# Layer 1's first pass reads x a second time with columns on partitions; the norm's roots are spread by a matmul of ones with a diagonal

## The chip, the cores and the metric

One core of one Trainium2 chip runs the whole kernel. The time is device microseconds of one execution; lower is better. The engines are named as the profile names them: PE is TensorE's matmul stream, PEld its weight loads, DVE is VectorE, ACT is ScalarE, POOL is GpSimd, SP is SyncE, which issues the DMAs.

## What is computed

A trunk of two layers over 2048 positions of width 1024, all in float32. Only the start of layer 1 matters here:

```
h = rms_norm(x, a_norm_g)          # x * rsqrt(mean(x*x) + 1e-6) * g, per position
u, v, z = split(h @ w_in, 3)       # w_in is 1024 x 6144
```

After that come a gated mixing over chunks, an output projection, and a second layer with chunked attention. The change leaves all of that alone.

## The kernel before, in words

**Products.** A float32 product is written as three products of float32r halves: `mm3` (L110 to L114) multiplies high by high (L111), high by low (L112) and low by high (L113). `split` (L433) makes the halves: ACT casts the high half (L434), DVE subtracts it from the source to get the low half (L437). Each large product is a 2x2 block scheme with seven partial products, numbered `ph`, in the order `PH = (1, 2, 6, 5, 7, 4, 3)`.

**Steps.** Layer 1's input projection runs in steps `(n, ph, j)`: `n` is one of six column groups of `w_in`, `ph` a partial product, `j` one of eight pairs of row blocks (x has 16 blocks of 128 rows; block 2j is the upper one of pair j, block 2j+1 the lower). A step is one 128x512 product of 12 matmuls. In the first pass, `n == 0`, steps 0 to 15 (`ph` 1 and 2) do the product for `n` 0 and `n` 1 together, so 24 matmuls each; steps 16 to 55 do `ph` 6, 5, 7, 4, 3 with 12 each. `run_steps` (L659) walks the steps; at each step it runs the events of that step, then the products (`act`), then prepares the left operand of the step three later (`prep`, `LOOK = 3`), then the list `ts` (weight loads and weight sums). This order of the program gives priorities; the framework's scheduler sets the order on each engine from them, so an instruction can stand some places away from where the source has it. Every engine then works through its queue in order.

**Left operands of the first pass.** `block_norm` (L692) makes a normalised block of 128 rows in four parts: `load` (SP reads x, and once the gains `gab` copied to all partitions), `square` (ACT, L703, sum of squares by row), `power` (DVE adds epsilon, L709; POOL raises to -1/2, L710) and `scale` (DVE, L714, one instruction of 128x1024: row factor and gains). `block_a(j)` does it for block 2j into `ha`, `block_b(j)` for block 2j+1 into `hb`. `block_c` (L728) forms the sums of the scheme on POOL (L734 to L736); `prep0` forms one more (L753). Rows are on partitions, but a matmul needs columns of x on partitions, so `s_split` (L607) turns each half block with four TensorE transpositions into PSUM tile `t0` (L611), then splits that tile into a tile `S`. It also stores `S` to the scratch `hsd` in DRAM (L614), from which later phases reload it (L602). `s_split` is called for all seven `ph` and eight `j`: 56 times.

**What sets the order around it.** `norm_at` (L915) places the parts of a block at steps: `load` early, `square` and `power` at step s, `scale` at s+1. The first two blocks are done ahead of all (`first_two`); blocks `ha` 2 to 7 load at once, `hb` blocks follow every 7/4 steps. `block_c` comes 2 and `block_d` 4 steps after the square of `hb`. All DMAs go through SP's queue in order: x loads (L697), weights `rw` (L470), stores `hsd` (L614), stores `vd` of finished v (L638), reloads of `S` (L602). POOL also sums weight blocks for the scheme (`comb`, L445). Finished products leave PSUM by `evict` (L568): ACT copies for `ph` 1 (L574), DVE adds for the others (L570). 32 dummy matmuls (L879) run before the first product.

Of the kernel before, what the change touches and what calls it, by code (L numbers as in the profile page):

```python
# [9 lines left out]
F32 = mybir.dt.float32  # L10
F32R = mybir.dt.float32r
BF16 = mybir.dt.bfloat16
AF = mybir.ActivationFunctionType
# [4 lines left out]
P = 128  # L18
# [15 lines left out]
def trunk_kernel(  # L34
    ctx: ExitStack,
    tc: tile.TileContext,
    x: bass.AP,
    a_norm_g: bass.AP,
    w_a: bass.AP,
    ln_g: bass.AP,  # L40
# [343 lines left out]
    with ExitStack() as actx:  # L384
# [48 lines left out]
        def split(hi, lo, src, key=None):  # L433
            ins = nc.scalar.copy(hi, src)  # L434
            if key:
                in_order(key, ins)
            nc.vector.tensor_tensor(lo, src, hi.bitcast(F32), op=sub)  # L437
            return ins
# [167 lines left out]

        def s_split(ph, j, rows):  # L607

            pt = ptp[0].tile([P, 4, P], F32, tag="t0", name=f"t0_{ph}_{j}", bufs=4)
            for k in range(4):  # L610
                tpose(pt[:, k, :], rows[:, k * P : k * P + P], ident[:])  # L611
# [76 lines left out]
        gab = p0.tile([P, D], F32, name="gab")  # L688
        ha = {}
        h21 = {}  # L690

        def block_norm(blk, t):  # L692

            r = sm.tile([P, 1], F32, tag="rr", name=f"ra{blk}", bufs=4)

            def load():
                nc.sync.dma_start(t, x[blk * P : (blk + 1) * P, :])  # L697
                if blk == 0:
                    nc.sync.dma_start(gab[:], a_norm_g.partition_broadcast(P))

            def square():
                jk = ca.tile([P, D], BF16, tag="acc", name=f"jk{blk}", bufs=25)
                ins = nc.scalar.activation(  # L703
                    jk[:], t, AF.Square, scale=1.0 / 32, accum_out=r[:]
                )
                last["square"] = ins.ins.name

            def power():
                nc.vector.tensor_scalar(r[:], r[:], EPS, None, op0=add)  # L709
                ins = nc.gpsimd.tensor_tensor(r[:], r[:], mhalf[:], op=ALU.pow)  # L710
                last["power"] = ins.ins.name

            def scale():
                nc.vector.scalar_tensor_tensor(t, t, r[:], gab[:], op0=mul, op1=mul)  # L714

            return load, square, power, scale

        def block_a(j):
            h = ha[j] = p0.tile([P, D], F32, tag="ha", name=f"ha{j}", bufs=8)
            return block_norm(2 * j, h[:])  # L720

        hb = {}

        def block_b(j):
            h = hb[j] = p0.tile([P, D], F32, tag="hb", name=f"hb{j}", bufs=3)
# [12 lines left out]
        def block_d(j):  # L738
            s_split(5, j, hb.pop(j)[:, 0:512])
# [150 lines left out]
        def at(s, f_):  # L890
            events.setdefault(s, []).append(f_)
# [23 lines left out]
        def norm_at(load, s, block, j):  # L915
            todo = []

            def first():
                todo.extend(block(j))
                todo.pop(0)()  # L920

            ts.setdefault(load, []).append(first)
# [356 lines left out]
    with ExitStack() as bctx:  # L1279
# [716 lines left out]
```

## Time and profile before

| | us |
|---|---|
| median of 3 runs | 2656.24 |
| lowest and highest run | 2654.09, 2656.88 |
| span of the profiled execution, first to last instruction | 2652.0 |
| PE busy in it | 2608.0 |
| DVE, ACT, POOL busy | 1885.1, 1303.2, 897.2 |

The profile is one execution. It gives its span, not a device time of its own; the runs shown lie 2.1 to 4.9 us above that span. A busy time is the sum of the durations of an engine's instructions; matmuls overlap in their pipeline, so PE's real pace is read from the distance between the starts of two instructions in the timeline, not from a duration. In the timeline a row is: start, length, engine, line, operation, output and input, count; in brackets the idle time before it and what ended it.

### The profile page before, as it was taken

Reading aid. Unit: us, or ns where it says so; the run is one execution under the profiler, and the core shown is the slowest. Engines: PE = TensorE matmul, PEld = TensorE weight load, DVE = VectorE, ACT = ScalarE, POOL = GpSimd, SP = SyncE. Lnnn points to the kernel's source line nnn. Section 1 sums busy time; section 2 is a strip of 40 time slices with the busy share of each in tenths; the row PEclk is TensorE's granted clock in tenths of the full one; section 3 lists DMA queues with packets and bytes.
Section 4 is the critical chain, followed back from the end, with each engine's and each line's share of the span. In section 5 each row is a group of like instructions: output and inputs, shape, how many; then the busy total and the mean of one; then the engine's idle time right before and its main releaser. Section 6 shows DMA issues by size and latency. Waiting matters only on the chain. (4 is left out here: it accounts for less than half of the span.)

```text
span 2652.0 us, 37980 instructions
## 1 busy us (share of the span) xinstructions
PE 2608.0 (98%) x12960; PEld 2181.4 (82%) x12960; DVE 1885.1 (71%) x2944; ACT 1303.2 (49%) x2303; POOL 897.2 (34%) x874
## 2 busy tenths in 40 slices
PE   8999999999999999999989999999999999999997
PEld 7888888888888888888878878888888888888886
DVE  5655676865767667757767767777778777877677
ACT  5422243442533434343356456666666655666564
POOL 3611334142152322203234434344332232332245
PEclk9999999999999999999999999999999999999999
DMA  7898998989989869967776597778787666875667
GB/s 286 313 344 329 346 370 323 323 323 338 330 302 313 308 233 324 331 206 270 280 251 214 186 280 229 231 245 263 252 270 254 226 204 224 255 230 161 195 224 251
DMA packets 273856, 718.72 MB, mean 271 GB/s; under 512 B 28800, under 2 KB 68736, under 8 KB 273664
## 3 DMA queue, kind: packets, MB, share of 16 engines
q1 hardware_dynamic: 273664, 716.31, 78.4%
q8 instruction: 103, 1.69, 0.3%
q14 instruction: 89, 0.73, 0.1%
HBM read 531.12 MB, written 174.59 MB: 266 GB/s over the span
## 5 line engine op out<-in xcount | busy, mean ns | idle before, releaser
L111 PE MATMUL P<-T,S 128*128 128x512 f32 x1248 | 496.2, 398 | 2.1 <-ACT S L434 2.1
L112 PE MATMUL P<-T,S 128*128 128x512 f32 x1248 | 488.2, 391 | 1.1 <-DVE T L437 1.1
L113 PE MATMUL P<-T,S 128*128 128x512 f32 x1248 | 488.6, 391 | 0.0
L1417 POOL TENSOR_SCALAR pr<-pr,sl 128x640 f32<-128x640 f32 (+4 forms) x256 | 209.7, 819 | 530.4 <-DVE sl L1416 445.2
L111 PE MATMUL pj<-hh_b,wh_b 128*128 128x512 f32 x768 | 320.4, 417 | 0.0
L113 PE MATMUL pj<-hh_b,wl_b 128*128 128x512 f32 x768 | 305.0, 397 | 1.2 <-DVE wl_b L229 1.1
L112 PE MATMUL pj<-hl_b,wh_b 128*128 128x512 f32 x768 | 303.4, 395 | 0.1
L1413 ACT ACTIVATE pr<-pr,nm 128x640 f32<-128x640 f32 (+4 forms) x256 | 195.5, 764 | 188.1 <-DVE nm L1406 186.6
L113 PEld LDWEIGHTS P<-T,S 128*128 128x128 f32 x1248 | 234.9, 188 | 50.5
L111 PEld LDWEIGHTS P<-T,S 128*128 128x128 f32 x1248 | 235.5, 189 | 46.9 <-ACT S L434 2.3
L112 PEld LDWEIGHTS P<-T,S 128*128 128x128 f32 x1248 | 235.6, 189 | 46.1 <-DVE T L437 1.3
L1438 DVE TENSOR_TENSOR pt<-tp,pt 128x640 fp32r<-128x640 f32 (+4 forms) x256 | 188.4, 736 | 43.7 <-ACT pt L1437 41.1
L1406 DVE CUSTOM_DVE_ANT_0 pr<-s,bias 128x640 f32<-128x640 f32 (+4 forms) x256 | 187.9, 734 | 35.7 <-PE s L1398 29.8
L1437 ACT CAST pt<-tp 128x640 fp32r<-128x640 f32 (+4 forms) x256 | 159.0, 621 | 54.0 <-PE tp L1433 49.8
L1433 PE MATMUL tp<-ident,pr 128*128 128x128 f32 x1120 | 166.7, 275 | 8.6 <-DVE pt L1438 7.3
L113 PEld LDWEIGHTS pj<-hh_b,wl_b 128*128 128x128 f32 x768 | 144.7, 188 | 36.4 <-DVE wl_b L229 3.8
L1433 PEld LDWEIGHTS tp<-ident,pr 128*128 128x128 f32 x1120 | 130.7, 140 | 43.3 <-issue 13.7
L111 PEld LDWEIGHTS pj<-hh_b,wh_b 128*128 128x128 f32 x768 | 145.8, 190 | 18.1 <-ACT wh_b L228 1.6
L1458 PEld LDWEIGHTS pv<-pt,V 128*128 128x128 f32 x896 | 143.3, 189 | 20.8 <-DVE pt L1438 3.9
L112 PEld LDWEIGHTS pj<-hl_b,wh_b 128*128 128x128 f32 x768 | 145.8, 190 | 17.1 <-DVE hl_b L186 0.6
L1458 PE MATMUL pv<-pt,V 128*128 128x256 f32 (+3 forms) x896 | 154.5, 320 | 2.2 <-ACT pt L1437 1.1
L229 DVE TENSOR_TENSOR wl_b<-raw_b,wh_b 128x1024 fp32r<-128x1024 f32 x96 | 120.4, 1255 | 28.5 <-ACT wh_b L228 27.8
(294 smaller groups left out, 5725.9 us busy)
## 6 DMA issues: line engine op xcount, KB each, us to landing
S<-hsd SPq DMA_DIRECT2D x288, 512.0 KB, 5.3
rw<-in_w_a SPq DMA_DIRECT2D x108, 512.0 KB, 6.3
A<-ytd SPq DMA_DIRECT2D x72, 512.0 KB, 5.7
raw_b<-wk SPq DMA_DIRECT2D x72, 512.0 KB, 4.3
hsd<-S SPq DMA_DIRECT2D x56, 512.0 KB, 4.9
V<-vhd SPq DMA_DIRECT2D x56, 512.0 KB, 5.4
bias<-reld SPq DMA_DIRECT2D x64, 320.0 KB, 4.2
va<-vd SPq DMA_DIRECT2D x32, 512.0 KB, 5.5
```

The costliest lines, as they stand in the source:

```text
L111: first = mm(ps, lh, rh, start=first, stop=False)
L112: mm(ps, lh, rl, start=False, stop=False)
L113: mm(ps, ll, rh, start=False, stop=last)
L229: tv(wl[:], raw[:], wh[:].bitcast(F32), op=sub)
L1406: nc.vector.tensor_tensor_reduce(out=pr[:, c0:].rearrange("p (a b) -> p a b", a=nseg), in0=ps[:, :nseg, :w], in1=bias[:, c0:].rearrange("p ...
L1413: nc.scalar.activation(pr[:, c0:], pr[:, c0:], AF.Exp, scale=-1.0, bias=nm[:], accum_out=sl[:])
L1417: nc.gpsimd.tensor_scalar(pr[:, c0:], pr[:, c0:], sl[:], 1.0, op0=ALU.mult, op1=ALU.mult)
L1433: ins = tpose(tp[:, b, :], pr[:, b * P : (b + 1) * P], ident[:])
L1437: nc.scalar.copy(oh, tp[:, b0:5, :].rearrange("p a b -> p (a b)"))
L1438: nc.vector.tensor_tensor(pt[:, 2560 + o + b0 * P : 2560 + o + 640], tp[:, b0:5, :].rearrange("p a b -> p (a b)"), oh.bitcast(F32), op=ALU ...
L1458: mm(po[:, q0 * P : q1 * P], vtl[t, p][:, i, hs], rhs, start=(i == blocks[0] and j == 0), stop=(i == 7 and j == 1),)
```

## The change

The host hands over a second copy of x, `xt`, in which each block of 128 rows is stored with columns on partitions: partition p holds, for k = 0 to 7, column 128k + p of the block's 128 rows. The gains come as 128 x 8, column on partition.

- `s_split` no longer transposes: it splits the half block straight from SBUF. The tile `t0` and the 56 x 4 transpositions are gone.
- `square` still works on x with rows on partitions, since it sums along a row. For `ha` blocks 0 to 3 that copy of x goes to a tile of its own (`xn`, of the tag of `hb`, now 4 buffers for 3) and SP loads `xt` beside it. For the other 12 blocks x is loaded into the block's tile, squared, and then ACT issues a DMA that overwrites the tile with `xt`.
- The row factors must now lie along the free axis. After the -1/2 power, POOL scales the identity by them (`dg`, a 128x128 diagonal); `spread`, new, is one float32 matmul of a tile of ones with `dg`, which leaves in PSUM tile `rb` the 128 factors on every partition.
- `scale` is eight DVE instructions of 128x128 for one of 128x1024: block column k of the tile times its gain times `rb`.
- `norm_at` gets a place for `spread`, and `scale` comes one step later for blocks not made ahead; `block_c` and `block_d` move one step later with it.

```diff
         def s_split(ph, j, rows):
-            pt = ptp[0].tile([P, 4, P], F32, tag="t0", name=f"t0_{ph}_{j}", bufs=4)
-            for k in range(4):
-                tpose(pt[:, k, :], rows[:, k * P : k * P + P], ident[:])
             t = s_tile(f"S0_{ph}_{j}")
-            split(t[:, 0], t[:, 1], pt[:], "S")
+            split(t[:, 0], t[:, 1], rows.rearrange("p (k c) -> p k c", k=4), "S")
...
-        def block_norm(blk, t):
+        def block_norm(blk, t, xr=None):
             r = sm.tile([P, 1], F32, tag="rr", name=f"ra{blk}", bufs=4)
+            apart = xr is not None
+            xr = t if xr is None else xr
+            dg, rb = [], []
             def load():
-                nc.sync.dma_start(t, x[blk * P : (blk + 1) * P, :])
                 if blk == 0:
-                    nc.sync.dma_start(gab[:], a_norm_g.partition_broadcast(P))
+                    nc.sync.dma_start(ga[:], a_norm_g)
+                nc.sync.dma_start(xr, x[blk * P : (blk + 1) * P, :])
+                if apart:
+                    nc.sync.dma_start(t, xt[blk])
             def square():
...
+                if not apart:
+                    nc.scalar.dma_start(t, xt[blk])
             def power():
...
+                dg.append(p0.tile([P, P], F32, tag="dg", name=f"dg{blk}", bufs=2))
+                nc.gpsimd.tensor_scalar(dg[0][:], ident[:], r[:], 1.0, op0=mul, op1=mul)
+            def spread():
+                rb.append(ptp[0].tile([P, P], F32, tag="rb", name=f"rb{blk}", bufs=2))
+                mm(rb[0][:], ones[:], dg[0][:], start=True, stop=True)
             def scale():
-                nc.vector.scalar_tensor_tensor(t, t, r[:], gab[:], op0=mul, op1=mul)
+                for k in range(KD):
+                    c = slice(k * P, k * P + P)
+                    nc.vector.scalar_tensor_tensor(
+                        t[:, c], t[:, c], ga[:, k : k + 1], rb[0][:], op0=mul, op1=mul
+                    )
...
             ts.setdefault(load, []).append(first)
-            at(s, lambda: todo.pop(0)())
-            ts.setdefault(s, []).append(lambda: todo.pop(0)())
-            at(s + 1, lambda: todo.pop(0)())
+            at(s, one)
+            ts.setdefault(s, []).append(one)
+            if s < -1:
+                at(s + 1, one)
+                at(s + 1, one)
+            else:
+                ts.setdefault(s + 1, []).append(one)
+                at(s + 2, one)
...
-            at(e + 2, lambda j=j: block_c(j))
-            at(e + 4, lambda j=j: block_d(j))
+            at(e + 3, lambda j=j: block_c(j))
+            at(e + 5, lambda j=j: block_d(j))
```

More of the change, by code (lines that the diff above doesn't have):

```diff
@@ L687, in trunk_kernel @@
         ptp = [ptx.enter_context(tc.tile_pool(name="pt0", bufs=1, space=PSUM))]
-        gab = p0.tile([P, D], F32, name="gab")
+        ga = p0.tile([P, KD], F32, name="ga")
+        ones = p0.tile([P, P], F32, name="ones")
+        nc.gpsimd.memset(ones[:], 1.0)
         ha = {}
         h21 = {}
-        def block_norm(blk, t):
+        def block_norm(blk, t, xr=None):
             r = sm.tile([P, 1], F32, tag="rr", name=f"ra{blk}", bufs=4)
+            apart = xr is not None
+            xr = t if xr is None else xr
+            dg, rb = [], []
             def load():
-                nc.sync.dma_start(t, x[blk * P : (blk + 1) * P, :])
                 if blk == 0:
-                    nc.sync.dma_start(gab[:], a_norm_g.partition_broadcast(P))
+                    nc.sync.dma_start(ga[:], a_norm_g)
+                nc.sync.dma_start(xr, x[blk * P : (blk + 1) * P, :])
+                if apart:
+                    nc.sync.dma_start(t, xt[blk])
             def square():
@@ L711, in power, with hb_tile @@
                 last["power"] = ins.ins.name
-            def scale():
-                nc.vector.scalar_tensor_tensor(t, t, r[:], gab[:], op0=mul, op1=mul)
-            return load, square, power, scale
+                dg.append(p0.tile([P, P], F32, tag="dg", name=f"dg{blk}", bufs=2))
[3 more added lines that the diff above has]
+                mm(rb[0][:], ones[:], dg[0][:], start=True, stop=True)
+            def scale():
+                for k in range(KD):
[3 more added lines that the diff above has]
+                    )
+            return load, square, power, spread, scale
+        def hb_tile(name):
+            return p0.tile([P, D], F32, tag="hb", name=name, bufs=4)
         def block_a(j):
             h = ha[j] = p0.tile([P, D], F32, tag="ha", name=f"ha{j}", bufs=8)
-            return block_norm(2 * j, h[:])
+            return block_norm(2 * j, h[:], hb_tile(f"xn{j}")[:] if j < 4 else None)
         hb = {}
         def block_b(j):
-            h = hb[j] = p0.tile([P, D], F32, tag="hb", name=f"hb{j}", bufs=3)
+            h = hb[j] = hb_tile(f"hb{j}")
             return block_norm(2 * j + 1, h[:])
@@ L1967 @@
         "x": c(a["x"][0]),
-        "a_norm_g": c(a["a_norm_g"][0]),
+        "xt": c(a["x"][0].reshape(S // P, P, KD, P).transpose(0, 3, 2, 1).reshape(S // P, P, D)),
+        "a_norm_g": c(a["a_norm_g"][0].reshape(KD, P).T),
         "w_a": c(np.stack([quarters(m) for m in w_a])),
```

5 lines of the change are left out of this document (4 added, 1 removed).

## Prediction

> **What bounds the kernel now.** I read the page first, then the table of engines by stretches of time around the change, then the line of the transpositions with its timeline, and last the waits of the engines that feed TensorE there.
>
> ```profile
> span 2652.0 us, 37980 instructions
> PE 2608.0 (98%) x12960; PEld 2181.4 (82%) x12960; DVE 1885.1 (71%) x2944; ACT 1303.2 (49%) x2303; POOL 897.2 (34%) x874
> ```
>
> ```profile
> 0.00:10.00 10.00, 7.10 (x36) 6.66 (x36) 1.64 (x4) 4.34 (x6) 2.09 (x10) 1.00 0.77 281
> 10.00:28.00 18.00, 16.11 (x69) 12.63 (x69) 14.56 (x19) 14.54 (x27) 2.75 (x5) 0.91 1.01 398
> 28.00:40.00 12.00, 11.65 (x59) 9.66 (x59) 8.14 (x10) 4.55 (x9) 9.67 (x8) 1.00 0.12 46
> 40.00:56.00 16.00, 11.96 (x56) 9.95 (x55) 8.65 (x11) 8.46 (x14) 5.74 (x6) 0.89 0.98 357
> 56.00:72.00 16.00, 16.00 (x82) 13.38 (x81) 7.93 (x11) 8.38 (x15) 7.49 (x7) 1.00 0.77 292
> 72.00:88.00 16.00, 16.00 (x82) 13.41 (x81) 9.46 (x14) 8.95 (x16) 15.06 (x12) 1.00 0.85 305
> 88.00:104.00 16.00, 16.00 (x85) 13.49 (x83) 11.62 (x18) 4.85 (x9) 12.23 (x11) 1.00 0.73 241
> 104.00:122.00 18.00, 18.00 (x90) 15.00 (x89) 13.35 (x20) 9.76 (x16) 10.18 (x7) 1.00 0.95 359
> 170.00:236.00 66.00, 66.00 (x309) 54.56 (x308) 47.00 (x67) 24.05 (x36) 10.11 (x8) 1.00 0.93 323
> ```
>
> After the stretch come PE, PEld, DVE, ACT and POOL busy, then the clock, the DMA share and GB/s. TensorE is the bound: from 56 us on it is never idle, while DVE has a third of its time free. Only before 56 us does it wait. So an instruction taken out of TensorE's queue behind 56 us is time won, as long as nothing else becomes late. Two things are near their end: POOL in 72 to 88 (15.06 of 16) and the DMAs, whose highest rate here is 398 GB/s.
>
> **Removed: 224 transpositions.**
>
> ```profile
> L611 PE MATMUL t<-ident,ha x128: 270/272/328, 8.1 to 233.8; 128*128 128x128 f32 x128
> L611 PE MATMUL t<-ident,hb x64: 272/273/447, 28.5 to 123.0; 128*128 128x128 f32 x64
> L611 PE MATMUL t<-ident,h x32: 270/272/273, 147.3 to 170.1; 128*128 128x128 f32 x32
> ```
>
> ```profile
> 55.88 0.40 PE L111 MATMUL P<-T_hh,S 128*128 128x512 f32 x1
> ...
> 58.39 0.39 PE L113 MATMUL P<-T_hh,S 128*128 128x512 f32 x1
> 58.62 0.60 PE L611 MATMUL t<-ident,ha 128*128 128x128 f32 x4
> 58.97 0.48 PE L111 MATMUL P<-T,S 128*128 128x512 f32 x1
> 59.29 0.40 PE L112 MATMUL P<-T,S 128*128 128x512 f32 x1
> ```
>
> The durations (0.27) overlap, so I take starts. From 55.88 to 58.39 lie 11 steps of one matmul: 0.228 each. From 58.39 to 59.29 lie 0.90, in which two such steps (0.456) are matmuls; the other **0.444** is the group of four transpositions. 128 + 64 + 32 are 224, that is 56 groups: 56 x 0.444 = **24.9 us** of TensorE.
>
> **Added on TensorE: 16 matmuls of ones with a diagonal.** No float32 matmul that isn't a transposition or a float32r half stands in this trace. From below, it costs as much as one transposition of the same 128 columns, 0.444 / 4 = 0.111. From above, 0.74, what the slow group of four below takes from its start to the next. I take 0.4: the kernel itself needs three products of halves for one float32 product, and four transpositions (0.444) are the nearest row to three passes with their weight loads. 16 x 0.4 = **6.4 us** (1.8 to 11.8). The Trainium skill, "TensorE: Matmul & The Clock Gate", section "Terms", says the transpose mode is four times faster for FP32 than a matmul. By it each would cost 0.444, an estimate, and the sum below would be 0.7 us later; no row here shows it.
>
> **Added beside TensorE.**
>
> ```profile
> L714 DVE SCALAR_TENSOR_TENSOR ha<-ha,ra,gab x8: 1276/1285/2303, 6.8 to 36.6; 128x1024 f32<-128x1024 f32 x8
> L807 DVE SCALAR_TENSOR_TENSOR va<-va,lmv,lg x64: 732/745/1855, 348.0 to 933.4; 128x512 f32<-128x512 f32 x64
> L1438 DVE TENSOR_TENSOR pt<-tp,pt 128x128 fp32r<-128x128 f32 x16 | 4.6, 285 | 0.3
> L1417 POOL TENSOR_SCALAR pr<-pr,sl 128x128 f32<-128x128 f32 x16 | 6.8, 426 | 8.0 <-DVE sl L1416 7.3
> L437 DVE TENSOR_TENSOR S<-t,S 128x512 fp32r<-128x512 f32 x56 | 37.1, 685 | 13.0 <-ACT S L434 13.0
> ```
>
> DVE: eight operations of 128x128 with one operand in PSUM, like L1438, 0.285 each, so 2.3 for 1.285 (between 1.6 at 0.2 and 2.9 at 0.36, which L714 and L807 give when their line is drawn on to 128 columns). That is 1.0 more per block, 16 us in all, nearly all between 10 and 122 us, where the quoted stretches leave DVE 38 us free: nothing, except in 10 to 28 (14.56 of 18), which I count below. The low halves of `S` (0.685) read two SBUF tiles instead of PSUM and SBUF. L714, which did so before, stretches from 1.285 to 2.303 at worst; such stretching leaves the scale and comes to the 56 splits. I set it at nothing: DVE has the room. POOL: 16 diagonals at 0.426 are 6.8 us; hidden on average, not in 72 to 88.
>
> ```profile
> hb<-in_x SPq DMA_DIRECT2D x8, 512.0 KB, 6.6
> ```
>
> ACT: 12 DMA issues, each behind the square whose tile it overwrites. The square is the instruction ahead on the same engine, so the casts and copies behind wait little, and ACT is half idle from 56 us on. But each of these transfers starts only then, and DVE's first scale waits for it; behind that scale stand the adds that empty PSUM, and behind those TensorE. An x block took 6.6 us to land; square and scale are two steps apart, 24 matmuls or 5.5 us each. So 11 us cover 6.6, and this costs nothing while transfers stay under that. `block_c` and `block_d` come a step later, and with them their `hsd` stores in SP's queue; their tiles are first used in step 24 (`ph` 5), so nothing waits.
>
> **Start.** Before the first product SP loaded x, gains, x; now it loads x, xt, x, xt, so the weights come one 512 KB load later: 0.524 MB at 398 GB/s, 1.3 us. The chain of the first block loses a group of transpositions (0.44) and the wait for `gab` below, and gains the diagonal (0.43), the matmul (0.4) and 1.0 of scale.
>
> ```profile
> 6.76 1.28 DVE L714 SCALAR_TENSOR_TENSOR ha<-ha,ra,gab 128x1024 f32<-128x1024 f32 x1 [1.09 <-DMA gab<-in_a_norm_g]
> 10.82 0.50 PE L111 MATMUL P<-T,S 128*128 128x512 f32 x1 [2.07 <-ACT S L434]
> ```
>
> That is +0.3 for the chain beside +1.3 for the loads, and DVE now has two longer scales ahead of the first low halves. I take **+2 us** (-1, if the 1.09 is all that counts, to +5, if the two further xt loads of this stage, 2.6, push as well).
>
> **The DMAs.** Sixteen xt blocks less the `gab` copy are 15 x 0.524 = 7.9 MB, at 398 GB/s 19.8 us of transfers, before 122 us. The quoted DMA shares leave 24.5 us free there (10.6 of them in 28 to 40, at share 0.12). But 32 groups lie in that part, so it gets 32 x 0.444 - 6.4 = 7.8 us shorter: 16.7 us are left for 19.8. I count the missing **3 us** as waits of TensorE (0 to 13.6, below).
>
> **The stall that is there.**
>
> ```profile
> 51.10 1.09 PE L611 MATMUL t<-ident,hb 128*128 128x128 f32 x4 [4.04 <-DVE hb L714]
> 51.84 0.78 PE L111 MATMUL P<-T,S 128*128 128x512 f32 x1
> 52.41 0.63 PE L112 MATMUL P<-T,S 128*128 128x512 f32 x1
> ...
> 54.50 0.40 PE L111 MATMUL P<-T,S 128*128 128x512 f32 x1
> ```
>
> ```profile
> 45.43 1.05 ACT L434 CAST T<-rw 128x1024 fp32r<-128x1024 f32 x1 [10.35 <-DMA rw<-in_w_a]
> ```
>
> TensorE waited 4.04 for a normalised `hb`, then ran slowly: 51.10 to 52.41 is 1.31 where 58.62 to 59.29 is 0.67, and the five steps to 54.50 take 2.09 for 1.14, so 1.6 more. The block was late since its square stood on ACT behind a cast that waited 10.35 for weights. The transposition that waited goes, but the new matmul of the same block stands behind the same square. I leave this stall as it is (0 to -5.6).
>
> **Sum.** -24.9 + 6.4 + 2 + 3 = **-13.5 us**. The profiled span of 2652.0 becomes 2638.5; the median lies 4.2 above that span, and with that kept the forecast is **2642.7 us**.
>
> **Rivals.**
>
> ```profile
> POOL ra L710: 17.2, 14
> 36.59 2.30 DVE L714 SCALAR_TENSOR_TENSOR ha<-ha,ra,gab 128x1024 f32<-128x1024 f32 x1 [2.40 <-POOL ra L710]
> 91.36 1.28 DVE L714 SCALAR_TENSOR_TENSOR hb<-hb,ra,gab 128x1024 f32<-128x1024 f32 x1 [6.34 <-POOL ra L710]
> 106.00 1.06 ACT L703 ACTIVATE jk<-hb 128x1024 bf16<-128x1024 f32 x1 [4.54 <-DMA hb<-in_x]
> ```
>
> *Slower: TensorE waits for the roots.* Before, DVE's scale waited for the root, 17.2 us in 14 waits, up to 6.34 where POOL was full, and TensorE went on with other products. Now the matmul that spreads the roots stands in TensorE's own queue; behind it stand products that need nothing of it. If those 17.2 us and the 4.54 for `hb` become TensorE's, with three slow restarts at 1.6, that is 26.5 us: -13.5 + 26.5 gives **2669 us**. It decides from 18.8 us of such waits on. Against it: the matmul comes a step, some 5.5 us, behind the root in the program, more than all waits but one.
>
> *No difference: the DMAs have no room.* The free 10.6 us of 28 to 40 were free because SP's queue stood still; if it does so again and only ACT's few loads use them, 13.6 us are missing instead of 3: -24.9 + 6.4 + 2 + 13.6 = -2.9, **2653 us**. For it: 398 and 357 GB/s on both sides of the gap. Against it: ACT's DMAs do not stand in SP's queue. The Trainium skill, "DMA: Bandwidth & Descriptors", section "Issuing engines are not separate DMA queues", states that a second issuing engine saves only issue time, since all share the same 16 engines; that speaks for this rival, and this trace, with one hardware queue, cannot show it.
>
> *More gain.* The matmul costs as little as a transposition (1.8 for 16), the stall with its slow restart goes (5.6), no DMA is late: -24.9 + 1.8 + 2 - 5.6 = -26.7, **2629.5 us**.
>
> **How the numbers follow.** Forecast 0.50, slower 0.20, no difference 0.13, more gain 0.17. A measurement of this kernel tells some 0.2% from no change, 5.3 us. The forecast with its own bounds (2634 to 2652) gives nearly all to faster, 0.03 to no difference: faster 0.64, same 0.16, slower 0.20. The range runs from 2627, which takes in the larger gain and its lower bounds, to 2667, where the rival on the other side has most of its price; some 0.18 is left out.
>
> **What would show it.** Right: no L611; in steps without waits one product of 12 matmuls follows the other with no gap of 0.44; the ones matmul at 0.4 from start to start; TensorE still full from about 60 us. Wrong: idle time of PE in front of the spread matmul with POOL's `dg` as releaser (first rival); casts or scales that wait for `xt` or `rw` with DMA share near 1 (second); a first product later than 13 us. The size fails if the ones matmul costs much over 0.74, or if DVE's eight operations take over 2.9 and the low halves come late.

## The result and the profile after

| | us |
|---|---|
| changed kernel, median of 6 runs | 2670.16 (2662.77 to 2677.24) |
| kernel before, median of 6 runs beside them | 2656.56 (2654.09 to 2660.67) |
| ratio, with its 95% interval | 1.0051 [1.0038, 1.0065] |
| span of the profiled execution, changed and before | 2665.9 and 2652.0 |

The change makes the kernel 0.5% slower, 13.6 us. The forecast was 2642.7. The rival "Slower: TensorE waits for the roots" had named 2669; how much of that agreement is luck is said further down.

The page of the changed kernel, its head:

```profile
span 2665.9 us, 37763 instructions
PE 2596.3 (97%) x12768; PEld 2167.2 (81%) x12768; DVE 1912.5 (72%) x3056; ACT 1304.8 (49%) x2303; POOL 908.7 (34%) x891
```

TensorE has 192 instructions less (224 transpositions gone, 32 new: each matmul of ones is two) and 11.7 us less busy time, but the span is 13.9 longer. So it idles more. Its stretches of time, with columns as before:

```profile
10.00:28.00 18.00, 11.50 (x43) 8.59 (x44) 13.90 (x39) 10.78 (x16) 2.48 (x6) 0.81 1.00 391
28.00:40.00 12.00, 11.50 (x55) 9.22 (x54) 9.75 (x39) 9.20 (x19) 4.96 (x10) 1.00 0.99 356
...
56.00:72.00 16.00, 11.83 (x43) 9.32 (x43) 13.64 (x24) 7.49 (x13) 11.22 (x8) 0.79 0.77 281
72.00:88.00 16.00, 16.00 (x74) 13.23 (x73) 6.94 (x17) 8.98 (x15) 11.34 (x11) 1.00 0.77 290
88.00:104.00 16.00, 12.05 (x50) 9.57 (x50) 16.00 (x27) 5.82 (x11) 9.42 (x9) 0.93 0.87 311
104.00:122.00 18.00, 12.91 (x51) 10.36 (x50) 12.84 (x23) 7.92 (x13) 17.92 (x14) 0.88 0.84 306
...
170.00:236.00 66.00, 57.86 (x245) 46.54 (x244) 45.99 (x62) 22.90 (x34) 17.41 (x13) 0.97 0.91 330
```

Where TensorE had been full from 56 us on, it now has holes: 11.83 of 16, 12.05 of 16, 12.91 of 18, 57.86 of 66. In the second of these stretches DVE is busy all the time, in the third POOL nearly so (17.92 of 18). The clock falls below 1 in the same stretches. The idle DMA time of 28 to 40 us (share 0.12 before) is used: 0.99. What TensorE waited for in the first 330 us:

```profile
PE rb L724 <- POOL dg L720: 18.0, 7, 5.1
PE P L112 <- DMA S<-hsd: 8.4, 5, 3.4
PE P L112 <- ACT S L435: 5.3, 2, 5.1
```

Total, number of waits, longest. Before, no `S` reloaded from `hsd` was late and there were no diagonals. The third row is the start: 5.06 of it stands in front of the first product. Of the 18.0 for the diagonals, 2.8 lie there too. One such wait in TensorE's timeline, and what comes behind it:

```profile
61.72 0.39 PE L114 MATMUL P<-T_hh,S 128*128 128x512 f32 x1
66.28 0.80 PE L724 MATMUL rb<-dg,ones 128*128 128x128 f32 x2 [4.17 <-POOL dg L720]
66.72 0.77 PE L112 MATMUL P<-T,S 128*128 128x512 f32 x1
67.30 0.63 PE L113 MATMUL P<-T,S 128*128 128x512 f32 x1
...
69.86 0.63 PE L113 MATMUL P<-T,S 128*128 128x512 f32 x1
```

The product behind the spread needs nothing of it, yet stands 4.17 us. Then TensorE runs slowly: from 67.30 to 69.86 lie six steps, 0.427 each where the prediction read 0.228. The granted clock was half in that time, and again soon after the stop of 3.95 us that ended at 100.78 (columns as before, the clock third from the end):

```profile
64.31:71.14 6.83, 4.86 (x13) 3.90 (x14) 4.47 (x11) 0.81 (x2) 5.72 (x5) 0.50 0.72 275
101.86:105.27 3.41, 3.41 (x10) 2.63 (x9) 3.41 (x8) 1.32 (x3) 3.33 (x4) 0.50 0.88 358
```

POOL shows why the diagonal was late:

```profile
59.14 3.92 POOL L773 TENSOR_TENSOR ha<-ha 128x512 f32<-128x512 f32 x1 [5.85 <-DVE S L438]
63.02 1.00 POOL L717 TENSOR_TENSOR ra<-ra,mhalf 128x1 f32<-128x1 f32 x1
64.00 1.87 POOL L754 TENSOR_TENSOR h<-ha,hb 128x512 f32<-128x512 f32 x1
65.85 0.37 POOL L720 TENSOR_SCALAR dg<-ident,ra 128x128 f32<-128x128 f32 x1
```

The root waited for a sum that itself had waited 5.85 for a low half on DVE and then took 3.92 instead of 1.3, and between the root and its diagonal the scheduler put another sum (1.87). The wait at 100.78 (3.95 us) came from DVE:

```profile
88.51 3.48 DVE L438 TENSOR_TENSOR S<-hb,S 128x512 fp32r<-128x512 f32 x2
...
92.51 2.14 DVE L729 SCALAR_TENSOR_TENSOR hb<-hb,ga,rb 128x128 f32<-128x128 f32 x8
...
96.36 0.67 DVE L438 TENSOR_TENSOR S<-ha,S 128x512 fp32r<-128x512 f32 x1
...
97.56 0.14 DVE L716 TENSOR_SCALAR ra<-ra 128x1 f32<-128x1 f32 x1
```

The sum of squares was ready at 89.15 (ACT). DVE came to its epsilon only at 97.56, behind all that stood ahead of it in its queue; of these 8.4 us, about 2.1 are the excess of two low halves that took 1.74 each instead of 0.68, and 2.14 the eight scale operations of another block. The longest wait, 5.09 at 119.78, begins with a late load of x. The square of that block stood on ACT for it; POOL then had weight sums ahead of the root and one sum of 2.12 between root and diagonal:

```profile
114.02 1.06 ACT L708 ACTIVATE jk<-hb 128x1024 bf16<-128x1024 f32 x1 [5.01 <-DMA hb<-in_x]
```

Before, the same block was late by 4.54; the prediction shows that row.

**A ledger for all kernels.** I count the product matmuls of the first pass in TensorE's timeline, from 0, and read the starts of the first (number 0) and of number 1200; "the 288th" below is number 288, and so on. The time between them holds idle time (gaps of over 0.05 us) and busy time. 1200 x 0.228 = 273.6 of the busy time are products at full pace, 24.9 are transpositions or 16 x 0.23 = 3.6 spreads; what remains I call slow pace. The last two columns are the 1200th start against the kernel before, and the ratio of the measured times. Each row is one execution, and the span of that of the kernel before lies 4.6 us under its median; the ratios rest on many runs.

| kernel | first | idle | slow pace | 1200th, against before | time, ratio |
|---|---|---|---|---|---|
| before | 10.8 | 5.5 | 3.5 | | |
| changed | 16.4 | 23.8 | 11.8 | +10.9 | 1.0051 |
| a_dgfirst | 15.9 | 19.9 | 8.9 | +3.5 | 1.0031 |
| e_lag | 15.7 | 18.2 | 8.5 | +1.3 | 1.0016 |
| f_lagdg | 15.5 | 12.8 | 10.9 | -1.9 | 1.0005 |
| c_noroots | 11.1 | 20.5 | 8.5 | -4.5 | 1.0013 |
| g_ring | 15.4 | 12.0 | 9.6 | -4.0 | 0.9987 |
| h_nogain | 15.4 | 17.0 | 7.4 | -1.2 | 1.0023 |
| i_start | 11.7 | 19.4 | 6.4 | -3.6 | 1.0000 |
| k_actgain | 16.9 | 25.8 | 12.3 | +13.9 | 1.0069 |
| m_extra | 16.6 | 4.1 | 3.1 | +3.9 | 1.0026 |
| l_half | 17.8 | 10.6 | 8.7 | -4.1 | 0.9987 |
| o_ceiling | 10.8 | 15.7 | 10.3 | -7.9 | 0.9983 |
| n_best | 11.8 | 16.3 | 7.0 | -6.0 | 0.9983 |
| t_only | 15.8 | 14.2 | 10.4 | -0.7 | 1.0023 |
| p_psum | 11.9 | 11.4 | 7.7 | -10.1 | 0.9973 |
| r_all | 11.2 | 16.8 | 6.4 | -10.2 | 0.9973 |
| u_copy | 12.4 | 11.6 | 8.2 | -8.9 | 0.9986 |
| q_sbuf | 10.5 | 8.6 | 7.5 | +6.9 | 1.0033 |

For the changed kernel: 5.6 later start, 18.3 more idle, 13.0 less busy (21.3 less work, 8.3 more slow pace): +10.9. Its 23.8 of idle time are 15.2 for diagonals (18.0 less the 2.8 ahead of the first product), 8.4 for reloads and 0.2 at the start. The remaining 3.0 of the span's 13.9 come after the 1200th matmul. Nearly all rows have some us there that the ledger doesn't hold; where reloads are late once more at 317 to 325 us (f_lagdg, g_ring, o_ceiling, n_best, p_psum, r_all, u_copy) 1 to 5 us lie between the 1200th and the 1248th. The rest was not located.

### The profile page after: what moved, and what is told of

Its sections match the earlier page's. It is cut to its first block, busy times and chain, and to the rows that moved or that the text cites. A ratio compares the mean times of both kernels' runs of the same rounds, so it can differ in the third digit from the quotient of the medians.

```text
span 2665.9 us, 37763 instructions
## 1 busy us (share of the span) xinstructions
PE 2596.3 (97%) x12768; PEld 2167.2 (81%) x12768; DVE 1912.5 (72%) x3056; ACT 1304.8 (49%) x2303; POOL 908.7 (34%) x891
## 5 line engine op out<-in xcount | busy, mean ns | idle before, releaser
L112 PE MATMUL P<-T,S 128*128 128x512 f32 x1248 | 496.9, 398 | 16.0 <-DMA S<-hsd 10.6
L113 PEld LDWEIGHTS pj<-hl_b,wh_b 128*128 128x128 f32 x768 | 145.4, 189 | 16.3
```

The lines of the kernel that those rows point to most:

```text
L112: first = mm(ps, lh, rh, start=first, stop=False)
L113: mm(ps, lh, rl, start=False, stop=False)
```

## Experiments

### Whose wait is it? The order and the time of the roots

Theory W: the whole loss is TensorE's wait for late diagonals. Its rival D: the loss comes from what the second reading and the new DVE work do to everything, and the waits are only where it shows.

**a_dgfirst.** In `power`, the name that holds back POOL's sums of `block_c` (L754) is the diagonal's, not the root's, so nothing comes between the two.

```diff
-                last["power"] = ins.ins.name
...
-                nc.gpsimd.tensor_scalar(dg[0][:], ident[:], r[:], 1.0, op0=mul, op1=mul)
+                ins = nc.gpsimd.tensor_scalar(dg[0][:], ident[:], r[:], 1.0, op0=mul, op1=mul)
+                last["power"] = ins.ins.name
```

> Only the order on POOL differs: the first sum of block_c (L754) is tied behind the diagonal instead of behind the root. Theory W (TensorE stands still behind the matmul that spreads the roots because the diagonal comes late; 18.0 us in 7 waits in the changed kernel): in front of three of the long waits an L754 of 1.87, 1.26 and 2.12 us ran between root and diagonal, so about 5 us go: 2665 us. Theory D (the first pass lacks room on DMA and DVE, and the waits would only move to the products): no change, 2670 us within 2.

Measured 2665.48, ratio 1.0031 [1.0017, 1.0046], as W said, though the interval overlaps that of the changed kernel. The waits for diagonals fell to 12.0 us in 4.

**e_lag.** For the `hb` blocks, spread and scale come one step later, and `block_c` and `block_d` with them (`e + 4`, `e + 6`).

> For the eight hb blocks the spreading matmul comes one step (24 matmuls, 5.5 us) later in TensorE's queue, and scale, block_c and block_d one step later with it. Theory W: the three long waits at hb blocks (4.17, 3.95, 5.09 us) lie under 5.5 us and go, with three slow restarts of 1.6: about 18 us less, 2652 us. Theory D: 2670 us within 4, with the time found again as waits of products for S.

Measured 2661.38, 1.0016 [1.0006, 1.0025]: between the two. Waits for diagonals 6.6 us in 4.

**f_lagdg.** Both.

> Both edits together. Theory W: hardly better than the later matmul alone, since that already covers the lateness: 2651 us. Theory D: 2668 us.

Measured 2657.42, 1.0005 [0.9995, 1.0015]. The waits for diagonals are down to 2.3 us, yet the kernel only comes back to where it had been before the change.

**c_noroots.** The changed kernel without diagonals and spreading matmuls: one tile of ones, made once, stands for `rb`, so the row factors are left out.

```diff
+        mm(rb1[:], ones[:], ident[:], start=True, stop=True)
...
-                rb.append(ptp[0].tile([P, P], F32, tag="rb", name=f"rb{blk}", bufs=2))
-                mm(rb[0][:], ones[:], dg[0][:], start=True, stop=True)
+                rb.append(rb1)
```

> Leaves out the diagonals and the 16 spreading matmuls: one matmul of ones with the identity at the start fills rb with ones, and every scale multiplies by gain and 1, so the row factors are missing from the result. Squares, roots, both reads of x and all eight-piece scales stay. Theory W: all 18.0 us of waits, their slow restarts (about 5) and 16 matmuls (about 7) go: 2640 us. Theory D: only the matmuls go: 2663 us.

Measured 2658.78, 1.0013 [0.9999, 1.0026]: far from W's 2640. TensorE's waits in it, first 330 us:

```profile
PE P L112 <- DMA S<-hsd: 9.7, 6, 2.3
PE P L112 <- ACT x L575: 6.4, 2, 4.7
PE P L112 <- DVE c L571: 4.4, 2, 2.9
PE P L112 <- ACT T L435: 3.0, 1, 3.0
```

So W, with the later place of scale and sums that goes with it, explains the way from 1.0051 to 1.0005, and no more. With the roots gone TensorE idles nearly as long (20.5 us for 23.8), for others: reloaded tiles, evictions, casts. Something else makes these late. The stretch from 56 to 122 us, kernel before and f_lagdg, points to DVE (third of the busy times) and POOL (fifth):

```profile
56.00:122.00 66.00, 66.00 (x333) 55.28 (x332) 42.36 (x63) 31.94 (x55) 44.95 (x36) 1.00 0.83 301
```

```profile
56.00:122.00 66.00, 62.80 (x270) 50.30 (x268) 62.80 (x105) 36.29 (x60) 60.52 (x46) 0.97 0.90 342
```

### The ring of S tiles, the amount of DVE work, the start

All on top of f_lagdg. Theory R: the six `S` tiles and the way through `hsd` set the pace of `ph` 5. Theory V: VectorE has too many operations.

**g_ring.** `S` of `ph` 7 gets tiles of the tag of `hb`, which is free by then, so the ring is left to the reloads.

```diff
-            t = s_tile(f"S0_{ph}_{j}")
+            if ph == 7:
+                t = p0.tile([P, 2, 4, P], F32R, tag="hb", name=f"S0_{ph}_{j}", bufs=4)
+            else:
+                t = s_tile(f"S0_{ph}_{j}")
```

> On top of the later spread with the diagonal first (2657.4 us, ratio to the kernel before 1.0005). The eight split tiles of phase 7, which are only stored, come from the buffers of hb (free by then) instead of the ring of six S tiles that the reloads of phase 5 use. Theory R (store and reload pass through the same six tiles, and from step 24 on their DMA latency, not TensorE, sets the pace; TensorE waited 6.4 us there for S from hsd): about 5 us less, ratio 0.998 to 0.999. Theory V (VectorE is the bound of the first pass: 62.8 of 66 us busy from 56 to 122): no change, ratio 1.000 to 1.001.

Measured 2652.84, 0.9987 [0.9978, 0.9996]: R is right in its size, some 4 us. The waits for reloads in the first 330 us, f_lagdg first:

```profile
PE P L112 <- DMA S<-hsd: 8.9, 4, 3.3
```

```profile
PE P L112 <- DMA S<-hsd: 4.4, 3, 2.4
```

**h_nogain.** One DVE multiplication of 128x1024 by `rb` (read eight times) for the eight operations; the gains are left out.

> On top of the later spread with the diagonal first. Leaves out the gains of the first norm: one DVE instruction of 128x1024 multiplies a block by rb, read eight times over, for eight of 128x128. DVE gets back about 0.9 us per block, 14 us in all. Theory V: the waits of TensorE for adds and low halves (about 5.5 us from 95 to 141) go, ratio 0.998. Theory R: nothing, ratio 1.0005.

Measured 2663.24, 1.0023 [1.0012, 1.0033]: slower than f_lagdg, so V as stated falls. The operation did get shorter (1.21 us for 2.15), but DVE stays full: 16.00 of 16 us from 56 to 72, with 13 instructions for 22. Something makes each of them long. Why it is slower, beyond a wait of 3.00 for an ACT eviction at 33.08 that f_lagdg doesn't have, was not settled.

**i_start.** The first `T` casts behind the first `S` cast on ACT, their low halves behind the first scale on DVE.

> On top of the later spread with the diagonal first. Only the order at the start differs: the casts of the first weights stand behind the first cast of x on ACT, their low halves behind the first block's scale on DVE, so that DVE scales while the weights are still on their way. The first product should start at 13 to 14 us instead of 15.5 to 16.4, so 2 to 3 us less: ratio 0.9995. If the later stages set the end anyway (theory R or V), the 2 to 3 us are lost again by step 32: ratio 1.0005.

Measured 2657.56, 1.0000 [0.9987, 1.0012]: the first product starts at 11.7 for 15.5, but at the 24th nothing of it is left (+4.2 and +4.3 against the kernel before), and 1.7 us at the 1200th.

**k_actgain.** The gains on ACT in eight pieces, one DVE multiplication.

> On top of the later spread with the diagonal first. All of the computation is done: ACT multiplies the gains in eight pieces of 128x128 (about 0.3 each, 2.4 us a block), DVE multiplies by rb in one instruction. Theory V: DVE's 14 us outweigh ACT's 38, since ACT has some 6 of 16 us free there; 2 to 4 us less, ratio 0.999. If ACT's queue then makes casts and copies late: 3 to 8 us more, ratio 1.002 to 1.003.

Measured 2675.96, 1.0069 [1.0052, 1.0086]. TensorE waits 10.3 us for ACT's evictions (L575): ACT has no room for this.

### The DMA traffic

Theory D, here for the DMAs alone: the 8 MB more have no room. Two edits bear on it: the traffic alone added to the kernel before, and half of it taken from g_ring.

**m_extra.**

```diff
                 last["square"] = ins.ins.name
+                nc.scalar.dma_start(dx[blk][:], x[blk * P : (blk + 1) * P, :])
```

> The kernel before, plus one thing: behind each block's square ScalarE issues a copy of the same 512 KB of x into a spare place in device memory, 16 in all (8.4 MB), which nothing reads. Theory D (the first pass has no DMA time for a second reading): the traffic of the first 236 us of the kernel before is 74.7 MB at a share of 0.93 to 1.0 in nearly all stages, its only idle stretch (28 to 40 us) takes about 4 MB of the 8.4, the other 4 MB at 0.4 MB per us cost TensorE some 10 us: 1.003 to 1.004 of the kernel before. Theory R (DMA is not the limit; lateness comes from the engines' order, VectorE and the ring): 0.9995 to 1.001.

Measured 2663.11, 1.0026 [1.0017, 1.0035]. The traffic is not free, but its price stands elsewhere than D has it: the ledger has +5.8 at the first product and +3.9 from the 288th on, unchanged to the 1200th. The rest of its 6.9 us comes behind the 1200th and was not located. In the timeline of DVE the first scale waits 5.09 for its gains, where it had waited 1.09 before:

```profile
11.36 1.28 DVE L716 SCALAR_TENSOR_TENSOR ha<-ha,ra,gab 128x1024 f32<-128x1024 f32 x1 [5.09 <-DMA gab<-in_a_norm_g]
```

**l_half.** `xt[blk][:, 0:512]` for `xt[blk]`.

> As g_ring (diagonal first, second blocks one step later, S_7 out of the ring), but the second reading moves only the first 512 of each block's 1024 elements, and the scaling takes the columns of the other half from the first, so the second half of the second reading of x is left out; the amount of work of every engine is the same, and the DMA traffic is 4.2 MB less. Theory D: some 5 to 10 us less than g_ring, 0.995 to 0.997 of the kernel before. Theory R: as g_ring, 0.998 to 0.9995.

Measured 2652.45, 0.9987 [0.9977, 0.9998]: as g_ring, and not the 5 to 10 us less that D asked for. The two intervals leave room for some 3 us either way, and the first product of l_half comes 2.4 us later than that of g_ring while both are level at the 288th; so a price of 2 to 3 us for half of the traffic is not excluded.

**o_ceiling.** c_noroots, e_lag, g_ring and l_half together.

> Second blocks one step later, S_7 out of the ring, half of the second reading left out as in l_half, and also no diagonals and no spreading matmuls (the norm's roots are left out of the operands: rb is a matrix of ones). What is left of the change is the removal of 24.9 us of transpositions and the smaller scaling operations. If the waits for the roots, the ring and DMA are together the whole of what was lost: 2635 to 2640 us, 0.992 to 0.994. If VectorE and GpSimd beside each other set a floor of their own (theory V): 0.996 to 0.998.

Measured 2652.10, 0.9983 [0.9973, 0.9993]: hardly better. The ledger reaches -13.5 at the 288th matmul and has -5.9 at the 432nd; in between, TensorE waits 4.46 for a DVE eviction and 2.75 for a low half of `S`. So DVE comes back into question, for another reason than the number of its operations.

**n_best.** g_ring and i_start.

> g_ring plus the start of i_start (the first T casts behind the first S cast on ScalarE, the first low halves of T behind the first block's scaling on VectorE). Nothing left out. The start gained 1 to 3 us in i_start's first 120 us and lost it again to waits for reloaded S tiles; with the ring relieved it may keep it: 0.9975 to 0.998; if the pass is paced by something else (DMA, VectorE): as g_ring, 0.9985 to 0.999.

Measured 2651.45, 0.9983 [0.9972, 0.9994]. Of the kernels that leave nothing out it has the lowest ratio, below the kernel before (0.0017 of the time, 4.5 us) and below the changed one; g_ring and u_copy lie within its interval.

### Two operands in SBUF

What is long are the low halves. DVE's groups from 56 to 122 us, in the kernel before and in g_ring (busy, mean ns, idle before):

```profile
L437 DVE TENSOR_TENSOR S<-t,S 128x512 fp32r<-128x512 f32 x20 | 12.8, 682 | 5.9 <-ACT S L434 5.9
```

```profile
L438 DVE TENSOR_TENSOR S<-hb,S 128x512 fp32r<-128x512 f32 x12 | 14.9, 1263 | 0.3 <-ACT S L435 0.2
L732 DVE SCALAR_TENSOR_TENSOR hb<-hb,ga,rb 128x128 f32<-128x128 f32 x48 | 13.1, 338 | 0.0
L438 DVE TENSOR_TENSOR S<-ha,S 128x512 fp32r<-128x512 f32 x11 | 12.6, 1148 | 1.4 <-ACT S L435 1.4
```

The same subtraction of the same size takes 0.682 us with its source in PSUM, as the transpositions left it, and 1.15 to 1.26 in the mean with both in SBUF. The mean mixes two cases. Of the 56 low halves of the changed kernel, 28 have no POOL instruction beside them, and these take 0.67 to 0.69, as with PSUM; the other 28 take 0.67 to 1.79, 1.23 in the mean. The DVE rows shown above have one of each kind. The two of 1.74 from 88.51 run beside POOL's sums, and the one of 0.67 at 96.36 falls into a pause of POOL:

```profile
89.82 1.62 POOL L773 TENSOR_TENSOR ha<-ha 128x512 f32<-128x512 f32 x1
97.78 0.93 POOL L717 TENSOR_TENSOR ra<-ra,mhalf 128x1 f32<-128x1 f32 x1 [6.34 <-DVE ra L716]
```

So it is not the place of the source alone that costs, but the two engines side by side. POOL, which reads SBUF in nearly all it does here, is also longer: the sum of `prep0` 1.297 before (L753), 1.610 in g_ring (L776). Over all its 128x512 sums of this stretch the difference is smaller, 1.38 in the mean before and 1.54 in g_ring, since some of them were long before too. Theory C: DVE with two SBUF operands and POOL hold each other up, and that is the second cause. Theory O: it is the order and number of DVE's instructions, whatever each takes.

**p_psum.** n_best, with the low half made as the high half minus an idle PSUM tile, so that its true values are left out. It then doesn't read the rows either.

```diff
+            ins = nc.scalar.copy(t[:, 0], rows.rearrange("p (k c) -> p k c", k=4))
...
+            nc.vector.tensor_tensor(t[:, 1], t[:, 0].bitcast(F32), zb, op=sub)   # zb in PSUM
```

> n_best, but the low half of each S tile is the high half minus an idle PSUM tile (128 columns, read four times) in place of rows minus the high half: same engine, same count and size, the wait for ScalarE's cast kept, one operand in PSUM as in the kernel before; the low halves' values are left out. Theory C (two SBUF operands on VectorE and GpSimd's reads and writes hold each other up, and this fills VectorE): the low halves return to some 0.68 us, GpSimd's sums to 1.3, VectorE from 56 to 122 us falls by some 10 us, and 5 to 10 us more are gained: 0.995 to 0.9965 of the kernel before. Theory O (VectorE's order and the number of its instructions, whatever each takes): as n_best, 0.9975 to 0.999.

Measured 2650.78, 0.9973 [0.9963, 0.9983]. DVE's and POOL's groups from 56 to 122 us:

```profile
L623 DVE TENSOR_TENSOR S<-S,zt 128x512 fp32r<-128x512 f32 x26 | 17.1, 678 | 5.2 <-ACT S L619 5.1
```

```profile
L788 POOL TENSOR_TENSOR ha<-ha 128x512 f32<-128x512 f32 x8 | 11.3, 1418 | 0.3
```

DVE's half of the mechanism is there: 0.678 each. POOL's half is less clear: the sum shown was 1.467 in n_best, and all its sums of this stretch come down from 1.53 to 1.44, not to 1.3. The time is better than that of n_best by 0.0010, less than C said (5 to 10 us, 0.002 to 0.004) and less than the two intervals can tell apart, though the ledger gives it 4.1 us at the 1200th. It reaches -14.2 at the 528th; then reloads are late again, 0.87, 2.04, and 2.67 at 316.49.

**q_sbuf.** The kernel before, all transpositions kept, with the low half reading `rows` in SBUF.

> The kernel before, with all its transpositions, but the low half of each S tile reads the untransposed rows in SBUF where it read the transposed ones in PSUM (so both operands in SBUF; the low halves' values are left out). Theory C: the low halves take 1.1 to 1.4 us in the mean where they took 0.68, GpSimd's sums 1.5 to 1.8; VectorE has 23 us of room from 56 to 122 us in the kernel before, so the time rises little: 1.000 to 1.002. Theory O: the low halves stay at 0.68, 0.9995 to 1.0005.

Measured 2665.06, 1.0033 [1.0021, 1.0045]: more than C's 1.000 to 1.002.

```profile
L615 DVE TENSOR_TENSOR S<-hb,S 128x512 fp32r<-128x512 f32 x9 | 14.7, 1654 | 0.0
L615 DVE TENSOR_TENSOR S<-ha,S 128x512 fp32r<-128x512 f32 x8 | 9.9, 1242 | 3.7 <-ACT S L613 3.5
```

This one edit costs 9 us in a kernel whose DVE has 23.6 of 66 us free. Late normalised blocks are the place: TensorE waits 5.47 and 2.46 us for them, where the kernel before has one such wait of 4.04, and the ledger has 4.0 more of slow pace. The edit also lets POOL's sums in place wait for the low halves that read the same rows (8.7 us of POOL, L758); before they waited as long for the transpositions (7.4), so this is not the difference.

**r_all.** c_noroots, e_lag, g_ring, i_start and the low halves of p_psum.

> All reliefs at once: second blocks one step later, S_7 out of the ring, the start of n_best, no diagonals and no spreading matmuls (the roots are left out), and the low halves of p_psum (their values left out); the second reading is whole. Theory C: with the roots out of the way too the transpositions' 24.9 us come out but for the start and the reloaded S tiles: 0.991 to 0.994. Theory O: as o_ceiling, 0.997 to 0.999.

Measured 2648.58, 0.9973 [0.9963, 0.9982]: far from C, at the lower edge of O. Low halves at 0.678, TensorE's busy time 22.0 us under that of the kernel before, but 16.8 us idle: 6.7 for reloads up to the 1200th matmul, 4.5 for an ACT eviction at 31.30, 2.2 for a DVE eviction.

**t_only.** The changed kernel with the low halves of p_psum and nothing else.

> The changed kernel, plus only the low halves of p_psum (high half minus an idle PSUM tile; their values left out); order of the diagonal, times of the blocks, ring and start as changed. Theory C (the two SBUF operands are the largest single loss of the changed kernel, also behind the late diagonals): low halves at 0.68 us, GpSimd's L773 back near 1.3 us, the waits for the diagonals fall from 18 us to under 10, 7 to 10 us less than the changed kernel: 1.001 to 1.0025 of the kernel before. Theory W (the waits come from the order of the roots alone): they stay at 15 us or more, 1.004 to 1.0055.

Measured 2661.22, 1.0023 [1.0013, 1.0033], against 1.0051 unchanged. TensorE's waits and the sum that had taken 3.92:

```profile
PE rb L729 <- POOL dg L725: 10.4, 6, 3.5
```

```profile
L778 POOL TENSOR_TENSOR ha<-ha 128x512 f32<-128x512 f32 x7 | 9.0, 1295 | 0.4
```

Without the two SBUF operands nearly half of the waits for the roots go, with no change in their order, and 0.0028 of the time, 7.4 us. So the first cause hangs on this edit in part. The edit does two things at once, though. The low half no longer stretches, and it no longer reads the rows, so POOL's sums in place needn't wait for it (7.4 us in 3 waits in the changed kernel, one of them the 5.85 shown above). No run separates the two.

**u_copy.** n_best; ACT copies the rows of each `S` tile to PSUM and both halves are made from there.

```diff
+            pt = ptp[0].tile([P, 4, P], F32, tag="t0", name=f"t0_{ph}_{j}", bufs=2)
+            nc.scalar.copy(pt[:], rows.rearrange("p (k c) -> p k c", k=4))
+            split(t[:, 0], t[:, 1], pt[:], "S")
```

> n_best, with one more step: ScalarE copies the four columns' rows of each S tile into PSUM (two buffers), and the high and the low half are made from there, as in the kernel before behind its transpositions. Nothing left out. ScalarE gets 0.6 us more for each of 26 S tiles from 56 to 122 us, 16 us on 37 of 66; VectorE and GpSimd lose their stretch (10 us of VectorE there). If ScalarE has that room: as p_psum, 0.996 to 0.998. If it becomes late, as in k_actgain: 1.000 to 1.004.

Measured 2651.77, 0.9986 [0.9977, 0.9994], as n_best. The low halves are at 0.681, ACT is busy 47.8 of 66 us, and TensorE waits 3.56 for an eviction on ACT at 74.28: what DVE gains ACT gives away.

## Why the prediction was wrong

**Removed, 24.9 us: right.** From the 384th matmul to the 408th, without a wait in either, the kernel before takes 6.4 us (123.0 to 129.4), the changed one 5.4 (132.9 to 138.3): that is two groups of 0.444 and the rounding. r_all, with neither transpositions nor spreads, has 22.0 us less busy TensorE time than the kernel before, in spite of more stops. The work went as counted; the gain did not arrive.

**The matmul of ones, 6.4 us: too high.** Where nothing is waited for:

```profile
43.48 0.39 PE L114 MATMUL P<-T_hh,S 128*128 128x512 f32 x1
43.70 0.38 PE L724 MATMUL rb<-dg,ones 128*128 128x128 f32 x2
43.84 0.48 PE L112 MATMUL P<-T,S 128*128 128x512 f32 x1
44.16 0.40 PE L113 MATMUL P<-T,S 128*128 128x512 f32 x1
44.39 0.40 PE L114 MATMUL P<-T,S 128*128 128x512 f32 x1
```

From 43.48 to 44.39 lie 0.91, less three steps of 0.228 is 0.23: 3.6 us for 16, within the bounds. It is two matmuls of the kind of a transposition (0.111 each). The Trainium skill, "TensorE: Matmul & The Clock Gate", section "Terms", has the transpose mode four times faster for FP32, from which the prediction estimated 0.444; this trace has twice.

**TensorE's queue behind the spread, counted at nothing: the failed step.** The prediction had the mechanism as its rival, with 17.2 us of DVE's old waits, and set against it that the spread comes a step behind the root. The trace has 18.0 us of such waits. Eight more were lost to slow pace (11.8 for 3.5); the rival had 4.8. A step's distance was not enough since root and diagonal stand in POOL's queue, between sums, and epsilon in DVE's. The later spread with the diagonal first (f_lagdg) took back 0.0046 of the time, 12 us. Two signs that the prediction had named for being wrong showed: PE idle in front of the spread with `dg` as releaser, and a first product later than 13 us (16.4). That the rival's 2669 was hit so closely is luck: it had the mechanism, but its waits were too long (21.7 for the 15.2 behind the first product) and its spread too dear, while its start was too cheap (2 for 5.6) and the reloads (8.4) were missing, and such errors nearly cancel.

**"L714 stretches ... I set it at nothing: DVE has the room": the failed step behind it.** The prediction saw that the stretch would move to the 56 splits. It looked at DVE's share of free time; but what matters is what waits behind each low half, and what POOL does meanwhile. Taking the two SBUF operands out of the changed kernel gives 0.0028 of the time back (t_only, with the reservation made there), putting them into the kernel before costs 0.0033 (q_sbuf). The Trainium skill, "SBUF — State Buffer", section "Who interferes with whom", states that a DVE instruction with two SBUF inputs contends with a GpSimd instruction that reads SBUF, and one with at most one SBUF input does not (outside some fast modes). The rows agree: 1.15 to 1.65 in the mean against 0.68 here, 0.67 to 0.69 with both in SBUF where POOL does nothing, and 3.92 at worst against 1.3 on POOL.

**DVE's eight operations: right in size.** 2.15 per block for 2.3. **POOL's diagonal:** 0.376 in the median for 0.426, but up to 1.33.

**Start, +2 us (to +5): 5.6.** ACT casts `S` at 15.73, behind four weight casts that each wait for their load:

```profile
10.93 1.04 ACT L435 CAST T<-rw 128x1024 fp32r<-128x1024 f32 x1 [1.43 <-DMA rw<-in_w_a]
...
15.73 0.61 ACT L435 CAST S<-ha 128x512 fp32r<-128x512 f32 x1
16.25 1.05 ACT L708 ACTIVATE jk<-xn 128x1024 bf16<-128x1024 f32 x1
```

and DVE did its scales from 14.43, behind low halves of weights. Where the casts stand, not the loads alone, made it 5.6: in i_start, which reorders them, the first product starts at 11.7 us, +0.9.

**"their tiles are first used in step 24 (`ph` 5), so nothing waits": wrong, for a reason that it didn't look at.** The first four steps of `ph` 5 wait for nothing, so the later stores did no harm; and `ph` 5 comes later than before (154.7 us for 147.7), not sooner. But its steps have lost a group of transpositions each, and from the fifth on reloads are late, into `ph` 7 and 4, 8.4 us in all. The tiles of `ph` 7, which are only stored, and the reloads of `ph` 5 go through the same six `S` tiles. g_ring, which takes the first out of that ring, took back 4 us of time on top of f_lagdg and half of the waits for reloads.

**"this costs nothing while transfers stay under that": it cost DVE time.** Three scales of `hb` waited for `xt`, though none of the transfers issued from 40 us on took more than 8.6 us to land:

```profile
DVE hb L729 <- DMA hb<-in_xt: 9.7, 3, 3.5
```

The second rival had named such waits as its sign, at a DMA share near 1; from 72 to 88 us, where one of them stands (3.46 at 84.16), the share was 0.77. Behind it DVE is busy without a pause from 88 to 104 us. Whether the lateness at 97.56 follows from it was not tried; in f_lagdg, where scale comes a step later, no scale of `hb` waits for `xt`.

**DMA, +3: neither shown nor excluded.** The idle time of 28 to 40 us was used, and the rival "the DMAs have no room", with 13.6 us of missing room, falls with it. Half of the second reading makes no difference that the runs can tell (l_half against g_ring), but they can't tell some 3 us. In m_extra about half of the traffic's price stands at the start, by way of the gains copied to all partitions, which the changed kernel doesn't load.

**The old stall, 5.6, left as it is:** it is gone at that place, and others stand elsewhere.

**What stays open.** With the roots, the ring, the start and the two SBUF operands all out of the way (r_all) the time is 0.9973, while 24.9 us less work would be 0.991. The idle time left is for reloads, evictions on ACT and DVE and late casts; which single queue sets them was not tried. The prices of the causes can't be added up: f_lagdg and t_only relieve the same waits in part, and no run takes each cause out alone from the same start.

## What to carry to other kernels

A tile that moves from PSUM to SBUF can change the time of its readers: look at what GpSimd reads at that time before calling VectorE's free share room. An instruction that waits in TensorE's queue holds back all products behind it, and here the long stops were followed by some us at half clock; so put it as far behind its input as the slowest queue on the way (here POOL's) can be late. And work taken off TensorE shortens the steps: check the ring of buffers and the order of the loads at the new pace.

## What was not expected of the hardware

- A plain float32 matmul of 128x128 is recorded as two matmuls and two weight loads, and takes 0.23 us of TensorE's queue, twice a transposition.
- Two VectorE operands in SBUF: 0.67 to 0.69 us for 128x512 with GpSimd idle, as with one in PSUM, but 1.23 in the mean and up to 1.79 beside GpSimd's instructions in the changed kernel. GpSimd's sums went from 1.38 to 1.54 in the mean, at worst 3.92.
- A stop of 4 to 5 us costs TensorE more than the stop. Behind those that ended at 66.28, 100.78 and 119.78 the matmuls come at 0.427 for 0.228 while the granted clock is 0.50, from 64.31 to 71.14, from 101.86 to 105.27 and from 118.92 to 125.75. At 100.78 the first steps still take 0.23 to 0.31, and the slow ones begin 1 us later. A shorter stop need not do it: behind one of 2.10 at 228.44 the steps take 0.23.
